# Softmax division, squares' low parts and head sums moved from GpSimd to VectorE in a two-layer encoder trunk

## The chip, the core and the metric

The kernel runs on one core of a Trainium2 chip. A core has five engines that work side by side, each through its own queue in order: TensorE (PE in the profile, with its weight loads as PEld), VectorE (DVE), ScalarE (ACT), GpSimd (POOL) and SyncE (SP). They wait for each other through semaphores. The metric is the device time of one execution in microseconds (us).

## The reference

Two layers of a hybrid encoder over 512 positions of width 1024, all in float32. Each layer adds half a gated feed-forward block, an attention stage with three kinds of heads, a second half feed-forward block, and a gated per-layer embedding. The attention stage is what the change touches:

```python
u = rms_norm(h, mix_norm[i]); proj = u @ w_in[i]        # all head groups and three gates
# A, 16 latent heads: logits from a 64-wide and a 32-wide rotary part
probs = softmax(logits, axis=-1);            o_A = probs @ v
# B, 16 banded heads (|i-j| <= 128), bias and a sink logit per head
probs = softmax(concat([logits, sink]))[..., :span];  o_B = probs @ v
# C, 8 differential heads: two softmax maps each
attn = probs[:, 0] - lam * probs[:, 1];      o_C = rms_norm(attn @ v, subln) * (1 - lambda_init)
merged = sigmoid(g_a) * o_a + sigmoid(g_b) * o_b + sigmoid(g_c) * o_c
h = h + merged @ w_out[i]
```

## The kernel before, in words

Activations lie transposed (features on the 128 partitions, 512 positions along the free axis). Every product is made three times as precise as one pass by splitting both sides into a high and a low part: high times high, low times high, high times low. Weights come from HBM in chunks of 128x1024. In the attention stage a chunk is split so (`Weights.part`): ScalarE casts the high part (line 101, `whi`), ScalarE writes its negative into the low part's tile (line 104), and a DMA issued from GpSimd's queue adds the raw chunk to it (line 105, `wlo<-wraw`). Elsewhere VectorE subtracts (line 107).

The attention stage (`mix`) walks over the heads in the order A (16 latent), C (8 differential), B (16 banded); names such as `m0B8` mean layer 0, group B, head 8. For each head four blocks of 128 queries are worked off:

1. `logits`: TensorE makes the scores of a block (`s`). VectorE takes the row minimum (line 1011 for A; for B and C lines 1066 and 1124 also add the bias strip). ScalarE exponentiates and sums (lines 1013, 1068, 1126).
2. The sums are inverted on VectorE (lines 1017, 1075, 1132), for A every two blocks, for B all four at once, and `normalise` (line 943) multiplies the block of probabilities (`p`) by the inverse in place, one `tensor_scalar` for each block, on GpSimd. For C `normalise` is applied to the second map only, and line 1136 on VectorE combines it with the first.
3. `transposes`, one head later: TensorE transposes the probabilities (`t`, line 955), ScalarE casts them to the high part (`pth`, line 958), VectorE subtracts for the low part (`ptl`, line 959).
4. `values`: TensorE multiplies with the values (`o`). For C, ScalarE squares the output (line 1152) and casts the high part of the squares (line 1154), GpSimd subtracts for their low part (line 1155, `sql`), a product with ones sums the squares, and a head later ScalarE takes the root, VectorE inverts it and applies it (lines 1165 and 1166), and GpSimd adds the result to the merged tile (line 1167, `mg`).

Between these steps TensorE gets other products as filler: the projections of the heads to come and of the gates (`qa`, `ga`, `va`, `qc`, `kc`, `gc`, `vc`, `qb`, `gb`, `vb`), and at the end of B the output projection (`wo`). So TensorE's own queue holds, between the transposes of a head and the products with its values, a number of filler matmuls.

The program is recorded in the order of the text; the framework's scheduler then orders each engine's queue by data dependencies and by costs of its own, except where `keep_in_program_order` pins an instruction. Moving an operation to another engine therefore moves its neighbours too, on TensorE and ScalarE as well.

Of the kernel before, what the change touches and what calls it, by code (L numbers as in the profile page):

```python
# [12 lines left out]
F32 = mybir.dt.float32  # L13
F32R = mybir.dt.float32r
AF = mybir.ActivationFunctionType
ALU = mybir.AluOpType
# [166 lines left out]
def encoder_kernel(ctx: ExitStack, tc: tile.TileContext, ins, out):  # L183
    nc = tc.nc
# [22 lines left out]
    def S(name, dt=F32):  # L207
        return sb.tile([P, 512], dt, tag="slot", name=name, bufs=SLOTS)

    def tiny(name):  # L210
        return sb.tile([P, 8], F32, tag="tiny", name=name, bufs=16)
# [3 lines left out]
    def PS(name, kind=None):  # L215


        if kind is None:
            kind = CYCLE[turn[0] % len(CYCLE)]
            turn[0] += 1  # L220
        return psp.tile([P, 512], F32, tag="ps" + kind, name=name, bufs=BANKS[kind])

    def mm(ps, lhsT, rhs, start, stop):
        nc.tensor.matmul(ps, lhsT, rhs, start=start, stop=stop, skip_group_check=True)  # L224

    def mm3(ps, lh, ll, rh, rl, start, stop):
        mm(ps, lh, rh, start, False)
        mm(ps, ll, rh, False, False)
        mm(ps, lh, rl, False, stop)
# [492 lines left out]
    def mix(l, prep, p2):  # L722
# [77 lines left out]
        for s in range(KSETS):  # L800
            for e in range(2):
                r = slice(64, 128) if e == 0 else slice(0, 64)
# [20 lines left out]
        merged = [None] * KT  # L823
# [115 lines left out]
                vs.append(t)  # L939
            got["vc", j] = vs  # L940

        def normalise(pt, r):
            nc.gpsimd.tensor_scalar(pt, pt, r, 1.0, op0=ALU.mult, op1=ALU.mult)

        class Head:
            steps_after = later = ()
# [47 lines left out]
        class Mla(Head):  # L994
# [6 lines left out]
            def logits(self):  # L1001
                i = self.i
                qh, ql = got.pop(("qa", i))
                kh, kl = KA[(i // 2) % KSETS][i % 2]
                m, sums = tiny(f"{self.name}m"), tiny(f"{self.name}s")
                self.p = []
                for q in range(TB):
                    c = slice(q * P, (q + 1) * P)
                    ps = PS(f"{self.name}s{q}", "s")
                    mm3(ps, qh[:, c], ql[:, c], kh, kl, True, True)  # L1010
                    nc.vector.tensor_reduce(m[:, q:q + 1], ps, axis=AX.X, op=ALU.min)
                    pt = S(f"{self.name}p{q}")
                    nc.scalar.activation(pt, ps, AF.Exp, bias=m[:, q:q + 1], scale=-1.0, accum_out=sums[:, q:q + 1])
                    self.p.append(pt)
                    n = NORMALISE["Mla"]
                    if (q + 1) % n == 0:
                        nc.vector.reciprocal(sums[:, 5 + q - n:5 + q], sums[:, 1 + q - n:1 + q])
                        for x in range(q + 1 - n, q + 1):
                            normalise(self.p[x], sums[:, 4 + x:5 + x])
                    yield  # L1020
# [4 lines left out]
            def values(self):  # L1025
                i = self.i
                c = (i % 4) * P

                def gated(o):
                    j = i // 2  # L1030
                    merged[j] = S(f"{name}mg{j}")
                    nc.vector.scalar_tensor_tensor(merged[j], got.pop(("ga", j)), 1.0, o, op0=ALU.add, op1=ALU.mult)
                self.out64(i, [v[:, c:c + P] for v in got["va", i // 4]], gated)
# [65 lines left out]
        class Diff(Head):  # L1099
# [10 lines left out]
            def logits(self):  # L1110
                i = self.i
                qs, (ks, kl) = got.pop(("qc", i)), got.pop(("kc", i))
                m, sums, r = tiny(f"{self.name}m"), tiny(f"{self.name}s"), tiny(f"{self.name}r")
                p, self.p = {}, []
                for q in range(TB):
                    c = slice(q * P, (q + 1) * P)
                    bs = self.strip[:, (TB - 1 - q) * P:(TB - 1 - q) * P + T]
                    for e in range(2):
                        x = e * TB + q
                        ps = PS(f"{self.name}s{q}{e}", "s")  # L1120
                        mm(ps, qs[e][:, c], ks[e], True, False)
                        mm(ps, qs[e][:, c], kl[e], False, True)
                        pt = S(f"{self.name}p{q}{e}")
                        nc.vector.tensor_tensor_reduce(pt, ps, bs, op0=ALU.add, op1=ALU.min, scale=1.0,
                                                       scalar=BIG, accum_out=m[:, x:x + 1])
                        nc.scalar.activation(pt, pt, AF.Exp, bias=m[:, x:x + 1], scale=-1.0, accum_out=sums[:, x:x + 1])
                        p[q, e] = pt
                        n = NORMALISE["Diff"]
                        if e == 1 and (2 * q + 2) % n == 0:
                            c = slice(q + 1 - n // 2, q + 1)  # L1130
                            rr = r.rearrange("p (e q) -> p e q", e=2)
                            nc.vector.reciprocal(rr[:, :, c], sums.rearrange("p (e q) -> p e q", e=2)[:, :, c])
                            nc.vector.tensor_scalar(rr[:, 1, c], rr[:, 1, c], neg_lam[:, l:l + 1], None, op0=ALU.mult)
                            for x in range(c.start, c.stop):
                                normalise(p[x, 1], r[:, 4 + x:5 + x])
                                nc.vector.scalar_tensor_tensor(p[x, 0], p[x, 0], r[:, x:x + 1], p[x, 1], op0=ALU.mult, op1=ALU.add)
                                self.p.append(p[x, 0])
                        yield
# [4 lines left out]
            def values(self):  # L1143
                i = self.i
                c = (i % 2) * P
                po = PS(f"{self.name}o", "s")
                for kt in range(TB):
                    _, hi, lo = self.pt[kt]
                    v = got["vc", i // 2][kt]
                    mm3(po, v[:, c:c + P], v[:, 256 + c:256 + c + P], hi, lo, kt == 0, kt == TB - 1)  # L1150
                sq = S(f"{self.name}sq")
                nc.scalar.activation(sq, po, AF.Square)
                sq_hi, sq_lo = S(f"{self.name}sqh", F32R), S(f"{self.name}sql", F32R)
                nc.scalar.copy(sq_hi, sq)
                nc.gpsimd.tensor_tensor(sq_lo, sq, sq_hi.bitcast(F32), op=ALU.subtract)
                o = S(f"{self.name}og")
                nc.vector.scalar_tensor_tensor(o, got.pop(("gc", i)), 1.0, po, op0=ALU.add, op1=ALU.mult)

                def finish():
                    ss = PS(f"{self.name}ss", "s")  # L1160
                    mm(ss, ones_r, sq_hi, True, False)
                    mm(ss, ones_r, sq_lo, False, True)
                    r = S(f"{self.name}r")
                    nc.scalar.activation(r, ss, AF.Sqrt, bias=eps, scale=1.0 / P)  # L1164
                    nc.vector.reciprocal(r, r)
                    nc.vector.scalar_tensor_tensor(r, o, sub_gain[:, l:l + 1], r, op0=ALU.mult, op1=ALU.mult)
                    nc.gpsimd.tensor_tensor(merged[i], merged[i], r, op=ALU.add)
                self.later = (finish,)


# [355 lines left out]
```

## Time and profile before

| | |
|---|---|
| time, median of 3 runs | 2968.56 us (2968.51 to 2968.79) |
| the profiled execution's own time | 2968.8 us |
| its span (first to last instruction) | 2967.0 us |
| mean granted TensorE clock | 0.997 |
| attention heads of layer 0: A, C, B (us from the span's start) | about 430 to 720, 720 to 917, 917 to 1064 |
| the same of layer 1 | about 1910 to 2180, 2180 to 2385, 2385 to 2531 |

Busy time is the time in which an engine executes; its idle time matters only where TensorE in the end waits for it. The view of waits gives, for each engine, who ended its idle time and how long that took; the chain of waits follows the work that ended last back through what released it. Matmuls are pipelined, so two successive ones start closer together than each lasts.

### The profile page before, as it was taken

To read this page: it belongs to the slowest core of one execution; us is meant where nothing else is said; L and a number is where in the kernel's file an instruction comes from. 1 tells how busy PE (TensorE), PEld (TensorE's weight loads), DVE (VectorE), ACT (ScalarE), POOL (GpSimd) and SP (SyncE) were. 2 spreads that over 40 slices of the span, in tenths; PEclk is the share of its full clock that TensorE was granted. 3 is DMA by queue.
4 is the path that set the end of the run, shared out by engine and by line. 5 is a ranking of instruction groups with operands and counts; after the bars stand their busy time and mean duration, and the time that the engine had idled before them with its cause. 6 is when DMAs were issued, how large, how long until landed. Compare 5 with 4: busy or idle time off the path is not lost.

```text
span 2967.0 us, 45265 instructions
## 1 busy us (share of the span) xinstructions
PE 2917.5 (98%) x16812; PEld 2543.3 (86%) x16812; DVE 2118.4 (71%) x3659; ACT 1786.1 (60%) x3281; POOL 652.2 (22%) x856
## 2 busy tenths in 40 slices
PE   8999999999999999999999999999999999999998
PEld 7999878888888889999889998788888788899996
DVE  7777676645787768778687776765467876687776
ACT  5544457767788855445454454677578888544443
POOL 1131113322333331010211101133223333311103
PEclk9999999999999999999999999999999999999999
DMA  6585435455545557553356634344555465665532
GB/s 220 157 264 142 137 114 135 102 128 143 143 123 129 139 144 211 143 148 105 118 167 165 175 98 165 100 121 109 134 139 148 103 148 133 184 164 149 157 93 85
DMA packets 133932, 421.43 MB, mean 142 GB/s; under 512 B 16174, under 2 KB 18542, under 8 KB 133712
## 3 DMA queue, kind: packets, MB, share of 16 engines
q0 software_dynamic: 53712, 156.01, 26.2%
q1 hardware_dynamic: 78272, 260.64, 25.8%
q8 instruction: 132, 2.16, 0.3%
q10 hardware_dynamic: 1728, 1.90, 0.2%
q14 instruction: 88, 0.72, 0.1%
HBM read 331.39 MB, written 18.94 MB: 118 GB/s over the span
## 4 chain that ended last, share of the span: by engine, by line
PE 86%; ACT 5%; DVE 5%; issue 2%; DMA 1%; POOL 1%; DVEq 0%; ACTq 0%; SPq 0%; POOLq 0%
PE ffn21d L224 4%; PE ffn20d L224 4%; PE ffn10d L224 4%; PE ffn11d L224 4%; PE ple L224 3%; PE wo L224 2%; PE m1ga L224 1%; PE m0ga L224 1%; PE m1qb L224 1%; PE m1qc L224 1%; PE m0qc L224 1%; PE m0qb L224 1%; PE m0vc L224 1%; PE m1vc L224 1%; PE m0gb L224 1%
## 5 line engine op out<-in xcount | busy, mean ns | idle before, releaser
L101 ACT CAST whi<-wraw 128x1024 fp32r<-128x1024 f32 x312 | 326.6, 1050 | 261.7 <-issue 71.2
L107 DVE TENSOR_TENSOR wlo<-wraw,whi 128x1024 fp32r<-128x1024 f32 x166 | 204.1, 1233 | 107.2 <-ACT whi L101 98.8
L105 POOL DMA_DIRECT2D wlo<-wraw x146 | 127.2, 871 | 561.2 <-ACT wlo L104 470.6
L104 ACT ACTIVATE wlo<-whi 128x1024 fp32r<-128x1024 f32 x146 | 154.9, 1061 | 2.1
L554 DVE SCALAR_TENSOR_TENSOR x<-ffn10d,x 128x512 f32<-128x512 f32 x48 | 33.0, 688 | 34.1 <-PE ffn10d L224 34.0
L554 DVE SCALAR_TENSOR_TENSOR wo0h<-ffn11d,wo0h 128x512 f32<-128x512 f32 x48 | 33.0, 687 | 33.4 <-PE ffn11d L224 33.3
L554 DVE SCALAR_TENSOR_TENSOR wo0h<-ffn20d,wo0h 128x512 f32<-128x512 f32 x48 | 32.8, 686 | 31.1 <-PE ffn20d L224 31.1
L554 DVE SCALAR_TENSOR_TENSOR wo1h<-ffn21d,wo1h 128x512 f32<-128x512 f32 x48 | 32.8, 687 | 30.4 <-PE ffn21d L224 30.4
L367 POOL TENSOR_TENSOR f_1sq<-f_1sq,f_1sq 128x512 f32<-128x512 f32 x14 | 21.4, 1526 | 49.3 <-ACT f_1sq L362 49.0
L917 ACT CAST m1kc<-m1kc 64x512 fp32r<-64x512 f32 x32 | 18.6, 582 | 15.0 <-PE m1kc L224 13.5
L917 ACT CAST m0kc<-m0kc 64x512 fp32r<-64x512 f32 x32 | 18.6, 582 | 15.0 <-PE m0kc L224 13.5
L367 POOL TENSOR_TENSOR pg0sq<-pg0sq,pg0sq 128x512 f32<-128x512 f32 x7 | 10.6, 1512 | 71.0 <-ACT pg0sq L362 71.0
L367 POOL TENSOR_TENSOR pg1sq<-pg1sq,pg1sq 128x512 f32<-128x512 f32 x7 | 10.6, 1514 | 69.5 <-ACT pg1sq L362 69.5
L870 DVE SCALAR_TENSOR_TENSOR m1qc<-m1qc,m1qc 64x512 fp32r<-64x512 f32 x16 | 11.0, 689 | 18.9 <-ACT m1qc L869 18.8
L870 DVE SCALAR_TENSOR_TENSOR m0qc<-m0qc,m0qc 64x512 fp32r<-64x512 f32 x16 | 11.0, 688 | 18.9 <-ACT m0qc L869 18.7
L1164 ACT ACT_TABLE_LOAD x16 | 20.5, 1283 | 0.3
L738 POOL DMA_DIRECT2D h_dram<-x x8 | 4.4, 547 | 71.9 <-DVE x L554 71.9
L738 POOL DMA_DIRECT2D h_dram<-wo0h x8 | 4.4, 547 | 71.4 <-DVE wo0h L554 71.4
L938 DVE TENSOR_TENSOR m1vc<-m1vc,m1vc 128x256 fp32r<-128x256 f32 x16 | 6.4, 414 | 14.3 <-ACT m1vc L937 14.2
L938 DVE TENSOR_TENSOR m0vc<-m0vc,m0vc 128x256 fp32r<-128x256 f32 x16 | 6.4, 414 | 14.3 <-ACT m0vc L937 14.2
L869 ACT ACTIVATE m1qc<-m1qc 64x512 fp32r<-64x512 f32 x16 | 9.5, 592 | 10.4 <-PE m1qc L224 9.0
L869 ACT ACTIVATE m0qc<-m0qc 64x512 fp32r<-64x512 f32 x16 | 9.5, 591 | 10.4 <-PE m0qc L224 9.0
(15134 smaller groups left out, 12409.0 us busy)
## 6 DMA issues: line engine op xcount, KB each, us to landing
wraw<-in_wall SPq DMA_DIRECT2D x312, 512.0 KB, 3.4
wlo<-wraw POOLq DMA_DIRECT2D x146, 512.0 KB, 4.7
copies_s<-bias_s POOLq DMA_DIRECT2D x16, 256.0 KB, 9.8
copies_d<-bias_d POOLq DMA_DIRECT2D x8, 512.0 KB, 10.7
h_dram<-x POOLq DMA_DIRECT2D x8, 256.0 KB, 2.7
pp_dram<-m0ppt POOLq DMA_DIRECT2D x8, 256.0 KB, 3.7
wo0h<-h_dram POOLq DMA_DIRECT2D x8, 256.0 KB, 7.0
ple0p<-pp_dram POOLq DMA_DIRECT2D x8, 256.0 KB, 4.4
```

Source lines behind the costliest of these rows:

```text
L101: pin(self.nc.scalar.copy(hi, raw))
L104: self.nc.scalar.activation(lo, hi.bitcast(F32), AF.Copy, scale=-1.0)
L105: self.nc.gpsimd.dma_start(lo.bitcast(F32), raw, accum_op=ALU.add)
L107: self.nc.vector.tensor_tensor(lo, raw, hi.bitcast(F32), op=ALU.subtract)
L224: nc.tensor.matmul(ps, lhsT, rhs, start=start, stop=stop, skip_group_check=True)
L367: self.engine.tensor_tensor(self.acc, self.acc, sq, op=ALU.add)
L554: nc.vector.scalar_tensor_tensor(h[d], ps, 0.5, h[d], op0=ALU.mult, op1=ALU.add)
L869: nc.scalar.activation(qs[e][own], ps[own], AF.Copy, scale=-0.125)
L870: nc.vector.scalar_tensor_tensor(qs[e][other], ps[own], -0.125, qs[e][own].bitcast(F32), op0=ALU.mult, op1=ALU.subtract)
L917: nc.scalar.copy(ks[e][r], ps[own])
L938: nc.vector.tensor_sub(t[:, 256:512], ps, t[:, 0:256].bitcast(F32))
L1164: nc.scalar.activation(r, ss, AF.Sqrt, bias=eps, scale=1.0 / P)
```

## The change

`normalise` gets a parameter for its engine, VectorE by default; heads A and B now use VectorE, and C names GpSimd and so stays where it was. The low part of the squares (line 1155) and the addition onto the merged tile (line 1167) of the C heads move to VectorE.

```diff
-        def normalise(pt, r):
-            nc.gpsimd.tensor_scalar(pt, pt, r, 1.0, op0=ALU.mult, op1=ALU.mult)
+        def normalise(pt, r, engine=nc.vector):
+            engine.tensor_scalar(pt, pt, r, 1.0, op0=ALU.mult, op1=ALU.mult)
...
-                                normalise(p[x, 1], r[:, 4 + x:5 + x])
+                                normalise(p[x, 1], r[:, 4 + x:5 + x], nc.gpsimd)
...
-                nc.gpsimd.tensor_tensor(sq_lo, sq, sq_hi.bitcast(F32), op=ALU.subtract)
+                nc.vector.tensor_sub(sq_lo, sq, sq_hi.bitcast(F32))
...
-                    nc.gpsimd.tensor_tensor(merged[i], merged[i], r, op=ALU.add)
+                    nc.vector.tensor_add(merged[i], merged[i], r)
```

Per layer that is 128 `tensor_scalar` (64 in A of 128x512; 64 in B, half of 128x256 and half of 128x384), 8 subtractions and 8 additions of 128x512. In all GpSimd's queue has 288 instructions fewer.

VectorE's queue in the banded heads, where head 9's probabilities are divided (layer 0; `ptl` is the low part of head 8's transposed probabilities):

```order
 L1075 RECIPROCAL m0B9s<-m0B9m 128x4
 L959 TENSOR_TENSOR m0B8ptl_10334<-m0B8t_10330,m0B8pth_10333 128x256
+L943 TENSOR_SCALAR m0B9p_10267<-m0B9p_10267,m0B9s 128x256
+L943 TENSOR_SCALAR m0B9p_10291<-m0B9p_10291,m0B9s 128x384
+L943 TENSOR_SCALAR m0B9p_10304<-m0B9p_10304,m0B9s 128x384
+L943 TENSOR_SCALAR m0B9p_10313<-m0B9p_10313,m0B9s 128x256
 L959 TENSOR_TENSOR m0B8ptl_10342<-m0B8t_10337,m0B8pth_10341 128x384
 L959 TENSOR_TENSOR m0B8ptl_10350<-m0B8t_10345,m0B8pth_10349 128x384
```

The four divisions of head 9 stand between the first and the second low part of head 8.

TensorE's queue at the same place, in the products with the values of head 8 (`B10s` are scores of head 10, `qb` and `gb` filler):

```order
 L224 MATMUL m0B8o<-m0B8pth_10341,m0vb_9053 128x384
 L224 MATMUL m0B10s_10387<-m0kb10h,m0qb_10270 128x256
 L224 MATMUL m0B10s_10387<-m0kb10l,m0qb_10270 128x256
-L224 MATMUL m0qb_10395<-m0u6h,whi_10162 128x512
+L224 MATMUL m0gb_10510<-m0u6h,whi_10277 128x512
+L224 MATMUL m0gb_10510<-m0u6h,wlo_10278 128x512
+L224 MATMUL m0gb_10510<-m0u6l,whi_10277 128x512
+L224 MATMUL m0gb_10510<-m0u7h,whi_10277 128x512
+L224 MATMUL m0gb_10510<-m0u7h,wlo_10278 128x512
 L224 MATMUL m0B8o<-m0B8ptl_10342,m0vb_9053 128x384
```

Ahead of the product that needs the second low part there are now five filler matmuls where there was one.

VectorE's queue in the differential heads, while the logits of C7 are worked off (`C4r` becomes head 4's normed output, `mg` the merged tile):

```order
 L1165 RECIPROCAL m0C4r<-m0C4r 128x512
-L883 TENSOR_TENSOR m0kb11l<-m0kb_8772,m0kb11h 64x512 x2
-L1166 SCALAR_TENSOR_TENSOR m0C4r<-m0C4og,sub_gain,m0C4r 128x512
 L1124 ISA m0C7p_8891,m0C7m<-m0C7s_8888,m0C7b 128x512
 L1124 ISA m0C7m 128x1
+L1166 SCALAR_TENSOR_TENSOR m0C4r<-m0C4og,sub_gain,m0C4r 128x512
 L870 SCALAR_TENSOR_TENSOR m0qb_8894<-m0qb_8816,m0qb_8894 64x512
+L1167 TENSOR_TENSOR m0mg_6093<-m0mg_6093,m0C4r 128x512
 L1124 ISA m0C7p_8923,m0C7m<-m0C7s_8920,m0C7b 128x512
```

The addition of head 4 now stands among the minima of head 7, behind the application of its norm.

## The prediction

> **What bounds the kernel now.** I read the page's busy times first, then the stages, then what TensorE waited for. The busy row, and the attention stages of both layers (A, C, B; A, C, B):
>
> ```profile
> PE 2917.5 (98%) x16812; PEld 2543.3 (86%) x16812; DVE 2118.4 (71%) x3659; ACT 1786.1 (60%) x3281; POOL 652.2 (22%) x856
> ```
> ```profile
> core 0: us, PE busy (x) PEld busy (x) DVE busy (x) ACT busy (x) POOL busy (x), PEclk, DMA share, GB/s
> 430.00:720.00 290.00, 286.75 (x1516) 242.94 (x1515) 169.94 (x304) 206.53 (x384) 81.37 (x103) 1.00 0.52 124
> 720.00:917.00 197.00, 191.00 (x1031) 161.96 (x1030) 146.41 (x284) 159.27 (x295) 62.67 (x76) 1.00 0.53 131
> 917.00:1064.00 147.00, 146.86 (x797) 123.51 (x796) 104.14 (x268) 120.95 (x280) 56.18 (x93) 1.00 0.56 135
> ...
> 1910.00:2180.00 270.00, 266.21 (x1416) 225.64 (x1414) 153.66 (x275) 190.47 (x353) 75.48 (x95) 1.00 0.52 124
> 2180.00:2385.00 205.00, 199.08 (x1059) 168.33 (x1058) 152.48 (x294) 164.55 (x304) 65.05 (x79) 0.99 0.54 131
> 2385.00:2531.00 146.00, 145.05 (x787) 121.64 (x786) 103.66 (x267) 120.34 (x280) 55.88 (x93) 1.00 0.57 135
> ```
>
> TensorE is the bound in all three stages: 286.75 of 290, 191.00 of 197, 146.86 of 147 us. VectorE has 59%, 74% and 71% of them, GpSimd 28 to 38%. A change that touches no matmul can only alter TensorE's idle time. What ended that time in layer 0 (engine that waited, whom for: us, times, longest):
>
> ```profile
> PE m0qb L224 <- DMA wlo<-wraw: 1.9, 1, 1.9
> PE wo L224 <- DMA wlo<-wraw: 1.2, 1, 1.2
> PE m0va L224 <- DVE m0ka11l L858: 1.2, 1, 1.2
> PE m0vc L224 <- DMA wlo<-wraw: 1.2, 1, 1.2
> PE m0C6o L224 <- DVE m0C6ptl L959: 1.2, 2, 0.7
> PE m0C0t L955 <- DVE m0C1m L1124: 0.9, 2, 0.5
> PE m0C4o L224 <- DVE m0C4ptl L959: 0.8, 1, 0.8
> PE m0C3t L955 <- DVE m0C4m L1124: 0.5, 1, 0.5
> ...
> PE m0va L224 <- DVE m0qa L850: 0.5, 1, 0.5
> ```
>
> No row names GpSimd's arithmetic. 5.1 us hang on VectorE, 4.3 on the weights' low parts. The engine that gets the work is the one TensorE waits for; the one that loses it is not. The moved division has cover too, as the next rows show: B8's blocks were divided from 989.5 to 991.1, its transposes began at 994.1. Nothing is therefore gained at the places that the diff names.
>
> **The price of one operation.** On GpSimd before, and the nearest VectorE rows:
>
> ```profile
> L955 PE MATMUL m0B8t<-ident,m0B8p x10: 270/271/273, 994.1 to 998.8; 128*128 128x128 f32 x10
> L943 POOL TENSOR_SCALAR m0A8p<-m0A8p,m0A8s x4: 683/690/1230, 546.9 to 552.9; 128x512 f32<-128x512 f32 x4
> L943 POOL TENSOR_SCALAR m0B8p<-m0B8p,m0B8s x4: 470/523/581, 989.5 to 991.1; 128x256 f32<-128x256 f32 x2, 128x384 f32<-128x384 f32 x2
> L1155 POOL TENSOR_TENSOR m0C4sql<-m0C4sq,m0C4sqh x1: 1293/1293/1293, 849.0 to 849.0; 128x512 fp32r<-128x512 f32 x1
> L254 DVE CAST warm<-one x1: 419/419/419, 7.9 to 7.9; 128x512 fp32r<-128x512 f32 x1
> L253 DVE CAST ones<-one x1: 219/219/219, 7.8 to 7.8; 128x128 fp32r<-128x128 f32 x1
> L1133 DVE TENSOR_SCALAR m0C1r<-m0C1r,neg_lam x2: 226/226/227, 734.7 to 740.0; 128x2 f32<-128x2 f32 x2
> L1074 DVE TENSOR_TENSOR m0B4m<-m0B4m,m0B4s x1: 163/163/163, 953.6 to 953.6; 128x4 f32<-128x4 f32 x1
> L367 DVE TENSOR_TENSOR f_0sq<-f_0sq,f_0sq x7: 686/692/693, 15.9 to 20.6; 128x512 f32<-128x512 f32 x7
> ```
>
> The two casts have one SBUF input, as the division has: 384 more columns cost 200 ns, so 0.52 ns per column and 152 ns fixed. A `tensor_scalar` on two columns takes 226 ns where a two-input operation on four takes 163, so the scalar read from a tile adds some 0.06. That gives 0.48 us for 512 columns, 0.42 for 384, 0.35 for 256, and 1.53 us for a banded head's four. Bounds for 512 columns are the bare cast's 0.42 and L367's 0.69, with two inputs, plus 0.06 (0.75); I take 0.48, since the cast's operand is of the division's kind. Subtraction and addition are L367's operation: 0.69 each.
>
> Per layer VectorE gets in A 64 x 0.48 = 31 us, in B 16 x 1.53 = 24 us, in C 16 x 0.69 = 11 us. Its share goes to about 69%, 80% and 88%. None of these adds to the time by itself; each counts where something that TensorE waits for stands behind it.
>
> [...]
>
> **The banded heads (B).** VectorE's queue now holds head 9's four divisions between head 8's first and second low part. The trace there (start, us, engine, line, operation; VectorE, then TensorE):
>
> ```profile
> 1000.50 0.69 DVE L236 TENSOR_TENSOR m0mg3l<-m0mg,m0mg3h 128x512 fp32r<-128x512 f32 x1 [2.63 <-ACT m0mg3h L235]
> ...
> 1001.41 1.69 DVE L959 TENSOR_TENSOR m0B8ptl<-m0B8t,m0B8pth 128x256 fp32r<-128x256 f32 x4
> ```
> ```profile
> 1002.51 0.40 PE L224 MATMUL m0qb<-m0u6h,whi 128*128 128x512 f32 x1
> 1002.75 0.34 PE L224 MATMUL m0B8o<-m0B8ptl,m0vb 128*128 128x384 f32 x1
> ```
>
> The four low parts take 1.69 us; by an even share the second is there some 0.9 us after 1001.41, about 1002.3, and is used at 1002.75: 0.45 us to spare. With 1.53 us put in front it is 1.08 late. But the queue of TensorE has five fillers there instead of one; a filler starts 0.24 after its forerunner (1002.51 to 1002.75), so four more cover 0.96. About 0.15 us stays per pair of heads: 8 pairs, 2 layers, **+2.4 us**. Bounds: nothing, if other shifts cover the rest; 1.08 x 16 = 17 us, if the fillers run out or arrive late. An even head's divisions fall where VectorE's low parts waited for ScalarE anyway:
>
> ```profile
> 990.60 0.56 DVE L959 TENSOR_TENSOR m0B7ptl<-m0B7t,m0B7pth 128x384 fp32r<-128x384 f32 x1 [0.77 <-ACT m0B7pth L958]
> ```
>
> The 0.77 and the like of it ahead of the next low part take up most of the 1.53, so these heads are charged nothing.
>
> **The differential heads (C).** Here VectorE is itself the chain. From the chain of waits (start, us, what):
>
> ```profile
> 882.61 0.69 DVE m0qb L870
> ...
> 886.25 0.70 POOL m0C7p L943
> ...
> 886.97 1.84 DVE m0C7p L1136 x2
> 888.81 0.60 DVE m0C6ptl L959
> ...
> 892.94 0.60 DVE m0C6ptl L959
> ```
>
> TensorE waits for these two low parts of C6. The addition of head 4 (0.69) now stands right behind the L870 at the head of this piece, and so shifts all of it. The subtraction stands earlier, ahead of C7's first minimum, where it may meet slack. I charge one addition at each of the three places where TensorE already waits in this way (C3t, C4o, C6o): 3 x 0.69 x 2 layers = **+4.1 us**. Bounds: nothing, if the scheduler's shifts absorb it; 6 heads x 1.38 x 2 = 17 us if both operations count in all heads behind the first two.
>
> **The latent heads (A).** Transposes come long after their division. Where TensorE waited it was for VectorE to empty a bank (`m0va`, 1.2 and 0.5). Two divisions of a pair of blocks (0.97) may stand in front; I take half, 0.48 x 2 waits x 2 layers = **+1.9 us**, bounds minus 3.4 (both waits of both layers vanish as the order shifts) to plus 3.9.
>
> **GpSimd's queue.** Its other task is to issue the weights' low parts:
>
> ```profile
> L105 POOL DMA_DIRECT2D wlo<-wraw x146 | 127.2, 871 | 561.2 <-ACT wlo L104 470.6
> ```
>
> It sat idle 561 us in front of these, 471 of them for ScalarE: the DMAs wait for line 104, not for the divisions queued ahead. I give the relief **0**; at best all three weight waits go in both layers, 2 x 4.3 = 8.6 us.
>
> **Sum.** 2.4 + 4.1 + 1.9 = 8.4 us on the profiled execution's 2968.8 (span 2967.0 and 1.8 around it), which is 0.2 above the median of the runs: 2968.6 + 8.4 = **2977.0 us**.
>
> **Rivals.** *Fillers absorb everything.* For it: B had 71% VectorE load, ScalarE 82%, and still no wait, because the scheduler puts fillers where they are needed, and does so again. Against it: in C TensorE's order hardly changes. Only A's two extra half waits remain: about 2970.5.
>
> *GpSimd free, weights earlier.* The mechanism is the one of the 8.6 us: DMAs issued earlier, the three weight waits gone, VectorE's additions covered. For it: GpSimd was busy a third of B; against it: the 471 us for ScalarE. 2968.6 - 8.6 = 2960.
>
> *VectorE becomes the bound in B.* 104 + 24 = 128 of 147 us leaves 19, and a wait for ScalarE such as the 2.63 us above in each of eight pairs would take 21. Then each pair costs its full 1.08: 2968.6 + 17 + 6 of C and A = 2992. Against it: the five fillers. It decides from 2.5 us for a head's four divisions on (0.45 spare, 0.96 of fillers, 1.08), or where the fillers come too early.
>
> *VectorE and GpSimd block each other.* A two-input VectorE operation beside GpSimd's division is longer:
>
> ```profile
> L1136 DVE SCALAR_TENSOR_TENSOR m0C1p<-m0C1p,m0C1r,m0C1p x4: 740/958/1182, 735.8 to 742.3; 128x512 f32<-128x512 f32 x4
> ```
>
> 740 ns alone, 1182 beside it. If a division on VectorE likewise held up, or was held by, the issue of a weight DMA (0.87 us each), each of B's 16 pairs could lose 0.87 more: 2977 + 14 = 2991. [...]
>
> **How the numbers follow.** A measurement of this kernel tells about 0.2% (5.9 us) from no change. Chances: the forecast 0.33 (most of it, 0.30, over 2974.5), fillers absorb 0.32, GpSimd free 0.15, VectorE the bound 0.12, blocking 0.08. Faster by over 0.2%: 0.15 less a little for a smaller gain, 0.13. Slower by over 0.2%: 0.30 + 0.12 + 0.08 = 0.50. Within: 0.37. Bounds of all terms together: -12 and +38; eight times in ten 2962 to 2996.
>
> **What would show it.** VectorE's `tensor_scalar` at 0.42 to 0.55 us for 512 columns, its busy time up by about 130 us (2 x 66), GpSimd's down by about 200 (64 x 0.69, 64 x 0.52 and 16 x 1.29, twice); TensorE's waits on `ptl` in C4 and C6 longer by 0.7 each, small new waits on `ptl` in the banded heads, weight waits unchanged. I am wrong if the waits on VectorE in C don't grow, if the weight waits vanish, if divisions take 0.75 or more, or if B grows by more than 10 us a layer.

## The result, and the profile after

The change makes the kernel slower: 2993.9 us (2990.75 to 2994.45) against 2968.56, a ratio of 1.008 (95% interval 1.0069 to 1.0092). The prediction said 2977.0 and a range of 2962 to 2996: direction and range hold, but the loss is 25.3 us where the sum gave 8.4. The range holds by bounds that were set for other causes, so that part is luck. The profiled execution took 2992.11 us, its span 2990.2, so 23.2 more than the span before.

The busy row of the page after, the moved operations, and the two rows for the weights' low parts (engine line waited for: us, times, longest; then GpSimd's issues: busy us, mean ns, idle us ahead of them and whom for):

```profile
PE 2927.4 (98%) x16812; PEld 2548.0 (85%) x16812; DVE 2218.5 (74%) x3947; ACT 1787.9 (60%) x3281; POOL 445.2 (15%) x568
```
```profile
L943 DVE TENSOR_SCALAR m0A8p<-m0A8p,m0A8s x4: 476/478/481, 548.3 to 553.9; 128x512 f32<-128x512 f32 x4
L943 DVE TENSOR_SCALAR m0B8p<-m0B8p,m0B8s x4: 346/382/417, 999.3 to 1000.2; 128x256 f32<-128x256 f32 x2, 128x384 f32<-128x384 f32 x2
L1155 DVE TENSOR_TENSOR m0C4sql<-m0C4sq,m0C4sqh x1: 691/691/691, 850.9 to 850.9; 128x512 fp32r<-128x512 f32 x1
```
```profile
PE wo L224 <- DMA wlo<-wraw: 13.7, 5, 3.2
PE m0qb L224 <- DMA wlo<-wraw: 1.8, 1, 1.8
...
PE m0C6o L224 <- DVE m0C6ptl L959: 1.0, 2, 0.7
...
PE m0vc L224 <- DVE m0vc L938: 0.9, 1, 0.9
PE m0C5o L224 <- DVE m0C5ptl L959: 0.9, 2, 0.6
...
PE m0C4o L224 <- DVE m0C4ptl L959: 0.8, 1, 0.8
...
PE m0B11o L224 <- DVE m0B11ptl L959: 0.3, 1, 0.3
```
```profile
L105 POOL DMA_DIRECT2D wlo<-wraw x146 | 126.6, 867 | 1101.2 <-ACT wlo L104 646.1 <-DVE m1qa L850 62.9 <-DVE m0qa L850 61.9
```

The operations cost what was forecast: 0.48 us for 512 columns, 0.69 for the subtraction. In the attention stages no wait on VectorE is longer than 1.2 us. The row that stands out is the first, the output projection (`wo`) waiting for low parts of w_out. The same row in the view of waits of before:

```profile
PE wo L224 <- DMA wlo<-wraw: 2.6, 2, 1.3
```

So 11.1 of the 23.2 us are waits for weights, at the end of the banded heads of each layer, a place where the diff changes nothing. The timeline there, for layer 0 after (GpSimd's issue of the third w_out chunk's low part, then TensorE around its first use) and before:

```profile
1036.96 0.86 POOL L105 DMA_DIRECT2D wlo<-wraw  x1 [9.58 <-ACT wlo L104]
```
```profile
1039.69 0.38 PE L955 MATMUL m0B12t<-ident,m0B12p 128*128 128x128 f32 x2
1042.43 0.74 PE L224 MATMUL wo<-m0mg4h,wlo 128*128 128x512 f32 x1 [2.37 <-DMA wlo<-wraw]
```
```profile
1048.08 0.88 POOL L105 DMA_DIRECT2D wlo<-wraw  x1 [0.45 <-ACT m0B13pth L958]
```
```profile
1052.72 0.47 PE L224 MATMUL wo<-m0mg4h,wlo 128*128 128x512 f32 x1
```

After, the chunk's load is issued 11 us sooner than before, and still comes too late, because TensorE's queue asks for it some 13 us sooner: the fillers that stood here before (`gb`, and the first products of `wo`) were spent at earlier heads, and head B12 is only at its transposes, where before it was B14. At 1030 us one `gb` matmul of layer 0 is left, where before 13 were. Even before there was nothing to spare: the load landed at 1052.68 and its first product started at 1052.72. What follows the wait costs too. Stretches of the same kernel (width, then busy us of PE, PEld, DVE, ACT, POOL with counts, granted clock, DMA share, GB/s):

```profile
1040.00:1042.40 2.40, 0.07 (x1) 0.00 (x0) 2.30 (x5) 1.64 (x4) 0.00 (x0) 1.00 1.01 229
...
1042.40:1044.00 1.60, 1.57 (x6) 1.27 (x6) 1.57 (x5) 0.75 (x3) 0.00 (x0) 0.54 0.45 105
1044.00:1045.80 1.80, 1.80 (x8) 1.40 (x7) 1.48 (x7) 1.79 (x6) 0.00 (x0) 0.50 0.57 225
1045.80:1047.00 1.20, 1.20 (x7) 1.02 (x6) 1.20 (x6) 0.48 (x1) 0.00 (x0) 0.94 0.00 0
```

For 3.4 us behind the wait TensorE is busy at half its clock (0.51 from 1042.43 to 1045.83), a loss of 1.6. Such a drop to 0.50 lasts 3.4 us each time in these two traces. Before, there is one of them (at 2375 us), after there are five (at 148, 1042.5, 2391, 2524 and 2572), which is 1.7 us against 8.5; both kernels have a longer one at the very end (0.50 too), where TensorE is all but idle. Three of the four more stand at waits for w_out (2.37, 2.14 and 3.23 us). The one at 148 us lies ahead of the attention heads, with no wait in front of it, in a stretch whose work the change doesn't touch.

By the busy rows, 13.3 of the 23.2 us are more idle time of TensorE and 9.9 more busy time. The waits for w_out (11.1) and the three drops at them (5.1) make 16.2; the drop at 148 us is 1.7 more. The other 5.3 were not itemised: some 2 are other waits, which came and went in all stages (`m0vc` and `m0C5o` above are new, `m0C3t` is gone).

To place time in a kernel whose queue is reordered, I use one measure below: TensorE's time up to a mark, less what its instructions up to there would take if each followed its forerunner at the median distance of its form in the kernel before. In layer 0, and at the end of the program, this lost time stands at (us):

| up to | before | after |
|---|---|---|
| 720 (end of A) | 26.6 | 27.9 |
| 917 (end of C) | 36.7 | 39.1 |
| 1030 (within B) | 40.0 | 42.4 |
| 1140 (behind the output projection) | 43.3 | 56.8 |
| end of the span | 84.2 | 107.2 |

In the middle of the banded heads no more is lost than before (3.3 us in both). Their end, with the output projection, costs 11.1 us more; all that follows, with layer 1, costs 9.5 more. About half of the 1.3 up to 720 arose ahead of the attention heads, where the clock fell at 148 us.

### The profile page after: what moved, and what is told of

It is laid out like the page before. It is cut to its first block, busy times and chain, and to the rows that moved or that the text cites. A ratio compares the mean times of both kernels' runs of the same rounds, so it can differ in the third digit from the quotient of the medians.

```text
span 2990.2 us, 44949 instructions
## 1 busy us (share of the span) xinstructions
PE 2927.4 (98%) x16812; PEld 2548.0 (85%) x16812; DVE 2218.5 (74%) x3947; ACT 1787.9 (60%) x3281; POOL 445.2 (15%) x568
## 4 chain that ended last, share of the span: by engine, by line
PE 85%; DVE 6%; ACT 4%; issue 3%; DMA 2%; POOL 1%; DVEq 0%; POOLq 0%; SPq 0%; ACTq 0%
PE ffn10d L224 4%; PE ffn21d L224 4%; PE ffn20d L224 4%; PE ffn11d L224 4%; PE ple L224 3%; PE wo L224 2%; PE m1ga L224 1%; PE m0ga L224 1%; PE m0qc L224 1%; PE m1qc L224 1%; DMA wlo<-wraw 1%; PE m0gb L224 1%; PE m1gb L224 1%; PE m1qb L224 1%; PE m0qb L224 1%
```

## The experiments

Two theories at first. *Load*: VectorE has more to do, so what the heads need comes later. *Order*: the scheduler, seeing the new costs, put TensorE's queue in another order, and that order is what costs. They are hard to tell apart as long as each edit changes both. So five of the kernels hold TensorE's whole queue to the order that it has in another kernel, by edges between successive instructions that set the order alone (`names` are TensorE's instructions in the other kernel's order). The other engines' queues are still ordered by the scheduler.

```diff
+        for a, b in zip(names, names[1:]):
+            if seen[a].engine == seen[b].engine:
+                tc.add_manual_dep(seen[b], a, mybir.DependencyInfo(mybir.DependencyClass.NoSync, ...), ...)
```

Times against the kernel before on the same chip:

| run | us | ratio (95%) | us more |
|---|---|---|---|
| e1: all moved, TensorE's order of before | 3010.78 | 1.0138 (1.0123 to 1.0154) | 41.0 |
| e2: all on GpSimd, TensorE's order of after | 2997.23 | 1.0089 (1.0072 to 1.0105) | 27.5 |
| e3: only C's subtractions and additions moved | 2988.43 | 1.0063 (1.0048 to 1.0078) | 18.7 |
| e4: only A's divisions moved | 2970.03 | 1.0 (0.999 to 1.0009) | 0.3 |
| e5: after, `wo` chunk by chunk | 2999.16 | 1.01 (1.0085 to 1.0115) | 30.2 |
| e6: after once more (see there) | 2995.46 | 1.0086 (1.0071 to 1.0101) | 26.5 |
| e7: before, `wo` chunk by chunk | 2978.43 | 1.0036 (1.0022 to 1.0051) | 9.5 |
| e8: only B's divisions moved | 2992.61 | 1.0078 (1.0063 to 1.0093) | 23.7 |
| e9: after, order held, w_out's low parts subtracted | 2988.28 | 1.0062 (1.0047 to 1.0077) | 19.2 |
| e10: one addition per layer moved | 2975.69 | 1.0022 (1.0012 to 1.0031) | 6.6 |
| e11: before, order held, w_out's low parts subtracted | 2969.31 | 0.9998 (0.9989 to 1.0008) | 0.2 |
| e12: only B's divisions moved, order of before | 2988.28 | 1.0062 (1.0045 to 1.0078) | 19.4 |

**e1 and e2: engines and order crossed.** e1 is the changed kernel with TensorE's order of before, e2 the kernel before with TensorE's order of after.

> All operations stand on VectorE as in the changed kernel, but TensorE's queue is held to the exact order it had before. Theory order (the 25 us come from the order the scheduler chose for TensorE, w_out's products ahead of their chunks at the end of the banded heads): within 8 us of the kernel before, 2968 to 2977, the weight waits of 2.4, 2.8 and 3.2 us gone. Theory load (VectorE's 100 us more delay the heads' chain): without the earlier fillers the low parts come late in every pair of banded heads, 2985 or more, TensorE waiting for VectorE's line 959.

> All operations stay on GpSimd as before, but TensorE's queue is held to the order of the changed kernel. Theory order: 2985 to 2996, as slow as the change, with the same weight waits near the end of the banded heads. Theory load: VectorE has its old load, so 2966 to 2972.

Neither theory stands alone. The first run came out as *load* had it and the second 1.2 us above the range of *order*; each theory missed the other run. With the old order the moved operations cost 41 us, more than in the changed kernel; with the new order and no operation moved, 27.5. Only the old order together with the old engines is quick. The views of waits, e1 first:

```profile
PE wo L224 <- DMA wlo<-wraw: 2.6, 2, 1.3
PE m0va L224 <- DVE m0qa L850: 2.2, 1, 2.2
...
PE m0B0o L224 <- DVE m0B1s L1075: 1.4, 1, 1.4
...
PE m0C4o L224 <- DVE m0C4ptl L959: 1.4, 2, 1.2
...
PE m0B13o L224 <- DVE m0B13ptl L959: 0.9, 1, 0.9
PE m0B5o L224 <- DVE m0B5ptl L959: 0.9, 1, 0.9
```
```profile
PE wo L224 <- DMA wlo<-wraw: 15.2, 5, 3.3
...
PE m0C3t L955 <- DVE m0C4m L1124: 2.4, 2, 2.0
...
PE m0B1t L955 <- DVE m0B2m L1066: 1.5, 1, 1.5
```

e1 has the weight wait of before and many short waits on VectorE, in all stages: its lost time in layer 0 grows against before by 6.7 us up to 720, by 2.7 more up to 917, by 9.2 more up to 1030. e2 has no more VectorE load than before and the weight waits of after, so these come from TensorE's order alone. It also has waits on VectorE that neither kernel has (`m0C3t` had 0.5 before), presumably because that order was made for other durations; its 27.5 us are not the price of the weight waits alone. Read together, the new order is the scheduler's answer to the load. It buys some 16 of e1's 41 us off, and pays for it at the end of B. What is left is the 25.

**e3, e4, e8: one part alone.** Each is the changed kernel with the other parts put back on GpSimd. What stays on VectorE:

```diff
 e4, only A:   normalise(self.p[x], sums[:, 4 + x:5 + x])              # line 1019, on VectorE
 e8, only B:   normalise(self.p[x], sums[:, 4 + x:5 + x])              # line 1077, on VectorE
 e3, only C:   nc.vector.tensor_sub(sq_lo, ...), nc.vector.tensor_add(merged[i], ...)
```

> Only the squares' low parts and the sums onto merged tiles are on VectorE (32 operations of some 0.7 us); all divisions stay on GpSimd. Its TensorE order in the banded heads is like the changed kernel's. Theory order: 2984 to 2994. Theory load: 22 us more of VectorE's time, none of it in the banded heads: the prediction's charge of 4 for C, 2970 to 2975.

> Only the latent heads' divisions are on VectorE; TensorE's order changes only inside the latent heads. Theory order and theory load agree on little: 2966 to 2972; theory port blocking (VectorE and GpSimd locking each other out) would see some 128 divisions beside weight DMAs: 2975 or more.

> Only the banded heads' divisions are on VectorE. TensorE's order in the banded heads and behind them is nearly that of the changed kernel. Theory order: 2984 to 2994, with the same waits of wo. Theory that the C additions alone set off the loss: 2968 to 2974.

A's 128 divisions are free. C's 32 operations alone cost 18.7, B's 128 divisions alone 23.7; together they don't add up to the change's 25. In e3 no operation of the banded heads was moved, and yet it loses at the same place as the change. Its waits, then two stretches (columns as above):

```profile
PE wo L224 <- DMA wlo<-wraw: 14.4, 5, 3.3
```
```profile
1036.00:1040.00 4.00, 1.27 (x8) 0.85 (x7) 3.84 (x9) 2.27 (x7) 0.32 (x1) 1.00 0.93 179
1040.00:1046.00 6.00, 5.56 (x21) 4.44 (x22) 3.42 (x10) 3.48 (x11) 2.59 (x5) 0.72 0.31 98
```

This price is not the price of its operations. 32 of them at 0.69 are 22 us of VectorE's time, and only two of the 16 in a layer fall into B.

**e10: as little as possible.**

```diff
-                    nc.gpsimd.tensor_tensor(merged[i], merged[i], r, op=ALU.add)
+                    (nc.vector if i == 7 else nc.gpsimd).tensor_tensor(merged[i], merged[i], r, op=ALU.add)
```

> The kernel before with one addition per layer (head C7's, 0.69 us) on VectorE, everything else on GpSimd. TensorE's order in the banded heads differs in some 690 places per layer from the kernel before, although no operation of the banded heads was touched. Theory order: 2975 to 2992 from that alone. Theory load: 2 x 0.69 us of VectorE's time at most, 2967 to 2971.

Two operations of 0.69 us in the whole program cost 6.6 us, and the weight wait is there again:

```profile
PE wo L224 <- DMA wlo<-wraw: 8.7, 3, 3.2
```

That is the lower end of what the theory of order allowed, and nearly five times the load. By that, most of it comes through the order; a run with this edit and TensorE's old order, which would show it directly, was not made.

**e12: what B's divisions cost without the new fillers.** As e8, with TensorE's order of before.

> Only the banded heads' divisions are on VectorE, and TensorE's queue is held to its order of before (one filler ahead of the second low part, not five). The prediction's own term for this: 1.08 us late per pair, 8 pairs, 2 layers, 17 us, so 2986. The trace of the first experiment (0.43 and 0.86 us per pair in its waits for the low parts) says 1.29 x 16 = 21 us, 2990. If the first experiment's loss came from the latent heads and from C instead, 2969 to 2976.

19.4 us, between the prediction's 17 and the 21 read from e1. One pair of heads in its timeline, VectorE and then TensorE:

```profile
1013.69 1.27 DVE L943 TENSOR_SCALAR m0B10p<-m0B10p,m0B10s 128x256 f32<-128x256 f32 x4
1014.88 0.55 DVE L959 TENSOR_TENSOR m0B9ptl<-m0B9t,m0B9pth 128x384 fp32r<-128x384 f32 x1
```
```profile
1014.42 0.39 PE L224 MATMUL m0gb<-m0u1h,wlo 128*128 128x512 f32 x1
1015.49 0.44 PE L224 MATMUL m0B9o<-m0B9ptl,m0vb 128*128 128x384 f32 x1 [0.68 <-DVE m0B9ptl L959]
```

The matmul starts 1.07 us behind its forerunner instead of 0.23: 0.84 lost, and 0.43 at the other head of the pair, 1.27 x 16 = 20 us. The same place after, where the scheduler has put five fillers in, two rows of each queue:

```profile
1010.01 1.26 DVE L943 TENSOR_SCALAR m0B9p<-m0B9p,m0B9s 128x256 f32<-128x256 f32 x4
1011.19 1.34 DVE L959 TENSOR_TENSOR m0B8ptl<-m0B8t,m0B8pth 128x384 fp32r<-128x384 f32 x3
```
```profile
1011.72 0.40 PE L224 MATMUL m0gb<-m0u7h,wlo 128*128 128x512 f32 x1
1011.96 0.34 PE L224 MATMUL m0B8o<-m0B8ptl,m0vb 128*128 128x384 f32 x1
```

No wait: 0.24 from filler to product. But each filler used here is missing later, and e8 with its new order (23.7 us) is no better than e12 without it (19.4): in the banded heads the scheduler's answer wins nothing. In A it does: up to the end of A in layer 0, e1 loses 6.7 us more than before, the changed kernel 1.3.

**e5, e7, e6, e9, e11: is it the supply of weights?** In the order after, two of the four sums of `wo` run through three chunks before the other two begin. If that alone made the chunks late, taking them in turn should help (e5; e7 is the control on the kernel before):

```diff
+                    traced = nc.cur_bb.bb.instructions
+                    start = len(traced)
                     mm3(sums[d], wh[:, c], wl[:, c], m[k][0], m[k][1], k == 0, k == KT - 1)
+                    for i in traced[start:]:
+                        if i.engine == mybir.EngineType.PE:
+                            if chain:
+                                tc.add_manual_dep(i, chain[-1], ...)
+                            chain.append(i.name)
```

> The changed kernel, with the products of the output projection's first four sums held to the order chunk by chunk (all four sums take a chunk before the next), so that they cannot run ahead of the chunks. Theory supply (most of the 25 us are waits for w_out's low parts, because two of the four sums run ahead through three chunks and so keep the buffers): waits of wo for a weight load fall from 8.4 us in layer 0 to 3 or less, 2970 to 2980. Theory no cover (the earlier fillers are missing at the end of the banded heads, whatever their order): those waits turn into others, on VectorE or ScalarE, 2986 or more.

> The kernel before with the same chunk by chunk order of the output projection. Its weight waits for wo are 1.2 us in layer 0. Theory supply: 2964 to 2970, since there is hardly a wait to take away. If the order chunk by chunk itself costs (products later, other waits), over 2972, and then the fifth experiment's time has to be read against this one.

It doesn't help: 2999.16. The order in turn costs 9.5 us even in the kernel before, and in e5 the weight waits on loads vanish from this stretch while others take their place:

```profile
PE m0B11o L224 <- DVE m0B12s L1075: 2.0, 1, 2.0
PE wo L224 <- DVE wlo L107: 2.0, 1, 2.0
PE m0B12o L224 <- ACT m0B12pth L958: 1.8, 1, 1.8
```

In this form the theory of supply is refuted. The heads are behind, and without `wo` to fill in TensorE waits for them directly. e6 was to bring the low parts sooner by a subtraction on VectorE.

> The changed kernel with TensorE's order as it is, but the low parts of six w_out chunks per layer are subtracted on VectorE (1.2 us each) instead of written by ScalarE and added to by a load: they are there some 6 us earlier. Theory supply: wo's waits for weight loads go from 8.4 us to 2 or less in layer 0, and 5 to 15 us come back, 2978 to 2988. Theory no cover or load: VectorE has 15 us more, 2992 to 3000.

Its edit counted chunks where the names count split pairs, and so met chunks that are not split there. Instruction by instruction it is the changed kernel, and its 2995.46 only repeats the 2993.9. e9 makes the edit at the right chunks, with TensorE's order held to that of after; e11 is its control on the kernel before. `halved` is set for six chunks of w_out in each layer.

```diff
+        if self.by_load and self.halved:
+            for c in (slice(0, 512), slice(512, 1024)):
+                self.nc.vector.tensor_tensor(lo[:, c], raw[:, c], hi[:, c].bitcast(F32), op=ALU.subtract)
+            return
```

> The changed kernel with TensorE's queue held to exactly its order, and the low parts of the six w_out chunks of a layer subtracted on VectorE in two halves (2 x 0.69 us) instead of ScalarE's copy and a load of 5 us. Here the edit meets the chunks of w_out, which the sixth experiment's edit missed. Theory supply: TensorE's waits of wo for low parts fall from 13.7 us in both layers to 4 or less, nothing takes their place, 2978 to 2986. Theory no cover (the heads are late, the fillers spent, the weights only the last of several waits): other waits come up, on line 959's low parts or ScalarE, 2989 to 2997.

> Control for the ninth: the kernel before, its own TensorE order held, and w_out's low parts subtracted on VectorE in the same way. Theory supply: only its two waits of 1.2 to 1.3 us go, 2963 to 2969. If VectorE's additional 16 us come back as waits for line 959, 2970 to 2980, and the ninth's time is read against this one.

e9 lies below the second theory's range and above the first's. Its waits (lines stand 9 further down in this kernel):

```profile
PE wo L233 <- DMA wlo<-wraw: 6.6, 2, 3.3
...
PE m1B12t L964 <- DVE m1B10op L995: 0.9, 1, 0.9
PE wo L233 <- ACT m1mg5h L244: 0.9, 1, 0.9
PE m1B12t L964 <- DVE m1B13m L1075: 0.8, 1, 0.8
```

The weight waits fall by 7.1 us, the time by 5.6 against the change. In layer 0 the lost time between 1030 and 1140 is 9.4 instead of 14.4; in layer 1 waits on VectorE and ScalarE come up in its place, as the second theory said. The two waits of 3.3 that stay are for the next chunk, which still comes by a load. So these late weights carry some 6 us of the loss by themselves. Of the 19.2 that stay, 6.6 are the two waits that the edit did not reach. That the rest belongs to an order that has spent its cover before the last heads are through fits the waits above, but no run takes it apart.

No kernel here beats the one before; e4 and e11 equal it. Not settled: whether some order suits the moved operations better than the scheduler's, and by which of its costs the scheduler chose it.

## Why the prediction was right in direction, and what it missed

- **The bound**: right. TensorE is at 98%. That the change "can only alter TensorE's idle time" was not: the loss is 13.3 us of its idle time and 9.9 of longer busy time, 6.8 of them the clock's short drops.
- **The price**: right. 0.48 us at 512 columns, and 2 x 0.346 + 2 x 0.417 = 1.53 for a banded head's four. The durations of the moved operations sum to 132 us as forecast, but VectorE's busy time rose by 100: in a row they overlap by about 0.08 each (0.40 from start to start at 512 columns), and the four of B take 1.27 in the rows above.
- **A, +1.9**: a little high. e4 gives 0.3, within its interval of 0.
- **C, +4.1**: the size too large, and none of the three places grew. C4o stayed at 0.8, C6o fell from 1.2 to 1.0, C3t vanished; C5o (0.9) and `m0vc` (0.9) took their place. The lost time in C of layer 0 grew by 1.1.
- **B, +2.4**: the mechanism at the place was right, the sum was not. Five fillers do cover the division (no wait at 1011.96), and without them it costs 19.4 us (e12) where the bound said 17. One step in it was wrong: "so these heads are charged nothing". The even head's division stands ahead of the odd head's low part, and without fillers that is the larger half, 0.84 of 1.27.
- **The step that failed**: "four more cover 0.96". Fillers were counted as cover that costs nothing. They are a fixed stock: `gb` and `wo` matmuls drawn forward are absent at B12 to B15, where TensorE then meets w_out's chunks too early. That term, missing from the sum, is 11.1 us of layer 0's lost time; most of the 9.5 us lost behind layer 0 has the same rows (waits for w_out of 5.3 us where there were 1.3, and two drops of the clock, 3.4). The bounds did name "if the fillers run out or arrive late", but with the price of the division (17), not with that of the stage's end.
- **GpSimd's queue, 0**: the wrong sign. GpSimd is freer (15%, idle 1101 us ahead of these issues), and the weight waits grew by 11.1 all the same, because the demand moved further (13 us at the chunk shown) than the supply (11). The rival *weights earlier* falls with it: this chunk's load was issued earlier, and no time was won.
- **Rivals**: *VectorE the bound in B* came close in time (2992) for another reason; its own mechanism is what e1 and e12 show, not the changed kernel. *Fillers absorb everything* holds up to 1030 and no further. For *blocking* (e4's expectation calls it port blocking; no run shows a port) two rows speak, one in each layer. Where A's first divisions on VectorE began 0.6 us after the issue of a weight load had begun, the issue took 1.17 us:

```profile
441.36 1.17 POOL L105 DMA_DIRECT2D wlo<-wraw  x1 [61.90 <-DVE m0qa L850]
441.96 0.88 DVE L943 TENSOR_SCALAR m0A0p<-m0A0p,m0A0s 128x512 f32<-128x512 f32 x2
```

None of the 146 issues of a weight load before took more than 0.92 us, and none of the other 144 after more than 0.90. It is 0.3 us at two places (441.36 and 1920.84 us), and e4, which has A's divisions on VectorE too, shows no cost (0.3 us, within its interval of 0). The 1182 ns that the prediction takes for it belong to an operation with two inputs beside GpSimd's division; beside the issue of a weight load the same operation took 741 (before, at 736.89 us).
- **What would show it**: "weight waits unchanged" was wrong, "B grows by more than 10 us a layer" came true in layer 0 with its end (11.1), and both point at the same missing term. The waits on VectorE in C grew from 4.0 to 4.6 us in layer 0, where the sum had 2.1 more.

## What to carry to other kernels

Where a scheduler orders the queues, an edit's price is not the price of its operations: follow every filler that it draws forward to the place where it is missing, and look there at what TensorE meets next. Hold the bound engine's queue to each of the two orders and cross it with the edit: two runs show whether load and order can be told apart. Here they could not simply be added (41.0 and 27.5 us crossed, 25.3 together). And read a change of half a per cent against a control as small as one addition: here that control alone moved the time by 0.2%.

## What was not expected of the hardware

Behind a wait of 2.37 us TensorE's granted clock was 0.50 to 0.54 for the next 3.4 us, while longer waits passed without: behind the waits that ended at 1074.67 (2.82 us) and 1095.09 (3.18 us) it stayed at 1.00.

```profile
1074.60:1078.00 3.40, 3.33 (x19) 2.81 (x20) 0.89 (x2) 0.75 (x2) 0.54 (x1) 1.00 1.03 411
...
1095.00:1098.50 3.50, 3.41 (x15) 2.83 (x16) 3.50 (x3) 1.48 (x3) 3.34 (x3) 1.00 0.70 228
```

The length of the wait alone does not decide it in these runs. e6 executes the same instructions in the same order on every engine; there the wait at the same matmul (`wo<-m0mg0h,wlo`, 2.68 us, ended at 1074.70) is shorter, and the clock fell behind it (first row). And one drop of the changed kernel has no wait ahead of it, only 2.75 us of matmuls on 33 of the 128 rows (second row); in the kernel before the same stretch ran at 1.00 (third row):

```profile
1074.90:1078.30 3.40, 3.40 (x13) 2.92 (x13) 0.88 (x2) 0.80 (x2) 0.54 (x1) 0.50 1.03 411
```
```profile
148.20:151.60 3.40, 3.40 (x17) 3.40 (x18) 2.25 (x5) 0.62 (x1) 0.00 (x0) 0.50 0.18 41
```
```profile
148.20:151.60 3.40, 3.40 (x26) 2.86 (x24) 3.35 (x7) 0.62 (x1) 0.00 (x0) 1.00 0.09 10
```

In e1, where no wait in the attention stages is longer than 2.2 us, the clock fell too: its means over 5 us were 0.76 from 455 us, 0.84 and 0.82 from 915, 0.66 from 2405 and 0.71 from 2425, and over the whole span 0.995, as in the changed kernel (0.997 before). So shorter waits did not keep the clock up here, and where a drop falls differs between executions of the same instructions (the changed kernel and e6). What sets a drop off was not shown.
